# The last projection groups of an attention layer: spread over four tiles instead of three

## The chip, the cores and the metric

The kernel runs on one core of a Trainium2 chip. The time is that of one execution on the device, in microseconds (us). The core has five engines that run side by side, each taking its instructions in the order written for it: TensorE (PE, matrix products; PEld is its weight load), VectorE (DVE), ScalarE (ACT), GpSimd (POOL), and SyncE (SP), which here issues all transfers between the chip's outer memory and the memory beside the engines. Products land in a small accumulator memory of eight banks, which PE writes and DVE and ACT read.

## The reference

The model is a two-layer encoder over 1024 tokens of width 1024. Only layer 0 matters here, a differential attention with 8 heads:

```python
h = _rmsnorm(x, norm_g) * (1.0 + scale) + shift
q, k, v, z = jnp.split(h @ w_in, ...)          # 1024 columns each; q and k get a rotary embedding
sc = einsum('bqhcd,bkhcd->bhcqk', q, k) * scale # two score maps c = 0, 1 for each head
p = softmax(sc)
p = p[:, :, 0] - lam * p[:, :, 1]
o = einsum('bhqk,bkhd->bqhd', p, v)
o = _rmsnorm(o, subln_g) * (1.0 - lambda_init)
y = (o * silu(z)) @ w_out                       # then x = x + gate * y
```

All of it is float32. The kernel splits each float32 operand into a rounded high part and a rest, and forms a product from three: high x high, high x rest, rest x high.

## The kernel before

**Tiles.** The attention of layer 0 runs head by head. A head has 8 tiles of 128 queries (numbered 0 to 7); 4 tiles make a half of 512 queries. For each tile `q_tile` (from line 859) forms two score maps of 128 x 1024 on PE (L869, `s`). For each map DVE takes the negated maximum (L415, `nm`) and ACT the exponentials with their sum (L417). DVE then combines the two maps into one (L877, `e`). The combined tile is turned by PE, 128 x 128 at a time (L398, `tr`), ACT and DVE copy it out as a high part and a rest (L400 `pth`, L401 `ptl`), and when two tiles are turned, PE multiplies them with the values (`pv`, 24 products of three kinds, L173 to L175). This follow-up work of a tile, the class `Tail`, runs one and two tiles behind its scores, so the pv products fall into the odd tiles.

**Projection groups as filler.** The projections of later heads are cut into groups of three products of 512 columns (`gen_half`, written `acc` in the trace). A group is one step of the generator `stream0`. A table of six numbers for each tile says how many groups are written at six places of it: place 0 before the turning that follows the first score map, 1 after it, 2 after the second score map, 3 after the turning of the previous tile, 4 between the two parts of pv, 5 behind them. `FILL0` is the table for heads 0 to 6, `FILL7` that of the last head, where 13 groups are left: 5 for the first half of the tokens and 8 for the second. They form the gate projection z of head 7. When a half is complete, `silu_gate` makes the gate from it: a tanh on ACT (L804, `zth`) and a combination on DVE (L805, `gz`).

**What is done beside it in the last head.** `extra0(i)` is called at the end of tile i. At the end of tile `Z_LAST` it runs the rest of the stream and gives up the token memory: the pools that hold the normed tokens `h0` (64 KB in each partition) and the projection's scratch are closed, and pools for the output projection (`xp`, `pw`) are opened in their place. Then it starts the loads for the first of seven block products of the output projection (the class `Seven`: `fetch_a` loads activations, `fetch_w` weights, both L1183; `split_a` and `split_w` make the high part on ACT, L1202 `oah` and `woh`, and the rest on POOL, L1203 `oal` and `wol`). `PRE0` says how many steps of these products (`Pre7.step`, written `oy`) run at the end of each tile from tile 4 on; each is three products of 512 columns. SP's loads here are held in program order.

**Normalization of a head.** When a half of a head is finished, ACT squares it (L934, `osq`), PE sums the squares (L949, `ssq`), DVE and POOL make the factor, and SP sends it out and back as a broadcast (L423 `bc_d`, L425 `bc_s`). For the second half of head 6 this falls at the end of tile 2 of head 7.

**Order.** The order of each engine's instructions is written by a scheduler from its own cost estimates. It follows the order of the program only roughly. `behind("S")`, `behind("V")`, `issue_after` and `in_turn` tie single instructions to others: the casts of the output projection are put behind the latest softmax instruction on ACT, for example.

Of the kernel before, what the change touches and what calls it, by code (L numbers as in the profile page):

```python
# [48 lines left out]
PRE0 = (0, 0, 0, 0, 1, 2, 2, 3, 2, 2, 2)  # L49
PRE1 = (0, 0, 0, 0, 0, 0, 0, 1, 1, 1, 1)  # L50
LAST1 = (((0, 1), 0, HF), ((2,), 0, HF), ((3,), 0, 256), ((3,), 256, HF))
Z_LAST = 2
FILL7 = ((0, 1, 2, 1, 1, 0),) + ((0, 1, 1, 1, 1, 0),) * 2
G_WAIT = 5
G1_AT = 7
VB = (3, 3)
# [25 lines left out]
def trunk(ctx: ExitStack, tc: tile.TileContext, A, out):  # L82
# [946 lines left out]
    def attn0(h, fills, extra=None, late=None):  # L1029

        def close(half, o_, zz):
            if late and half == 1:
                ctx_["late"] = late(o_, zz)
                return
            o = a0b.tile([P, HF], F32, name="o", tag="o", bufs=2)
            sq = a0b.tile([P, HF], F32, name="osq", tag="osq", bufs=4)
            head_out(o_, o, sq, h, half)
            subln(o, sq, zz, half, h, None)

        ctx_ = dict(pool=a0b, l=0, h=h, open=lambda half: None, close=close)  # L1040
        for qp in range(4):
            half = qp // 2
            if qp % 2 == 0:
                zz = first.pop(0) if first else sm.tile([P, 4], F32, name="zz")
            for t in range(2):
                fl = fills(qp * 2 + t)

                def fill(i):
                    if fl[i]:
                        stream0.step(fl[i])  # L1050

                def mid(c):
                    if c == 0:
                        fill(0)
                        if tails[0]:
                            tails[0].turn(1)
                        fill(1)

                if first:
                    e0 = first.pop()  # L1060
                else:
                    e0 = q_tile(h, half, (qp * 2 + t) % 4, zz, a0b, mid)
                    fill(2)
                    after_scores(fill, 3)
                side.tick()
                tails[:] = [tails[1], Tail(qp, t, e0, zz, ctx_)]
                if extra:
                    extra(qp * 2 + t)
        if late:
            run_tails(lambda i: extra(8 + i))  # L1070
            while hooks:
                hooks.pop(0)()
            return ctx_["late"]
# [223 lines left out]
    def extra0(i):  # L1297
# [3 lines left out]
        if i == 1:  # L1301
            sv0.fetch_w(0, 0)
        if i < Z_LAST:
            return
# [13 lines left out]

        if i == Z_LAST:
            stream0.step(99)  # L1320
# [66 lines left out]

    tail0 = attn0(NH - 1, lambda i: FILL7[i] if i <= Z_LAST else (0,) * 6, extra0, late0)
    SP.dma_start(k0["12"], oF[0][NH - 1, 0])
# [1067 lines left out]
```

## Time and profile before

| what | value |
|---|---|
| median of 3 runs | 1389.32 us (1387.46 to 1389.65) |
| profiled execution, its own time | 1386.7 us |
| its span, first to last instruction | 1384.8 us |
| granted TensorE clock, mean | 0.996 |
| PE busy | 1362.2 us, 98% of the span |
| DVE, ACT, POOL busy | 940.0, 736.5, 701.6 us |

A row of the busy view by stretch gives the stretch, its length, and the busy time with the number of instructions of each engine, then the granted clock, the share of the transfer engines and GB/s. A timeline row gives start, length, engine, line, operation, tiles out<-in, shapes, count, and in brackets the idle time of the engine before it with what ended that. The chain of waits is the work that ended last, followed back; its rows have start, length and what. On PE the rows overlap, since products are pipelined: in the chain a product of 512 columns has 0.23 us, in the timeline 0.39. All starts are in us from the first instruction.

### The profile page before, as it was taken

Reading aid. Unit: us, or ns where it says so; the run is one execution under the profiler, and the core shown is the slowest. Engines: PE = TensorE matmul, PEld = TensorE weight load, DVE = VectorE, ACT = ScalarE, POOL = GpSimd, SP = SyncE. Lnnn points to the kernel's source line nnn. Section 1 sums busy time; section 2 is a strip of 40 time slices with the busy share of each in tenths; the row PEclk is TensorE's granted clock in tenths of the full one; section 3 lists DMA queues with packets and bytes.
Section 4 is the critical chain, followed back from the end, with each engine's and each line's share of the span. In section 5 each row is a group of like instructions: output and inputs, shape, how many; then the busy total and the mean of one; then the engine's idle time right before and its main releaser. Section 6 shows DMA issues by size and latency. Waiting matters only on the chain.

```text
span 1384.8 us, 20703 instructions
## 1 busy us (share of the span) xinstructions
PE 1362.2 (98%) x7334; PEld 1145.7 (83%) x7334; DVE 940.0 (68%) x1324; ACT 736.5 (53%) x1356; POOL 701.6 (51%) x550
## 2 busy tenths in 40 slices
PE   8999999999999999999999999999999999999997
PEld 6788888888888888887887888888888888888886
DVE  7654788877777767778596977545566555555684
ACT  5532465665565656566648543445454454545554
POOL 5434263646575757465694143531141373834674
PEclk9999999999999999999999999999999999999999
DMA  9857644344444434525654246499343463566463
GB/s 345 264 178 230 204 116 140 104 145 107 152 131 144 136 120 134 156 69 186 222 189 167 62 145 212 154 283 281 109 117 111 110 214 124 191 219 217 150 241 122
DMA packets 149387, 232.07 MB, mean 168 GB/s; under 512 B 20641, under 2 KB 57633, under 8 KB 149282
## 3 DMA queue, kind: packets, MB, share of 16 engines
q1 hardware_dynamic: 149282, 230.74, 52.4%
q8 instruction: 58, 0.95, 0.3%
q14 instruction: 47, 0.39, 0.1%
HBM read 144.74 MB, written 61.81 MB: 149 GB/s over the span
## 4 chain that ended last, share of the span: by engine, by line
PE 85%; DVE 6%; ACT 3%; DMA 3%; issue 2%; POOL 1%; SPq 1%; POOLq 0%; DVEq 0%; ACTq 0%
PE s L2071 10%; PE acc L173 9%; PE acc L175 9%; PE acc L174 9%; PE tr L398 8%; PE s L869 8%; PE pv L173 4%; PE pv L174 4%; PE pv L175 4%; DMA ada<-in_ada_ss 2%; PE oy L173 1%; PE oy L175 1%; PE oy L174 1%; PE zacc L174 1%; PE zacc L173 1%
## 5 line engine op out<-in xcount | busy, mean ns | idle before, releaser
L400 ACT CAST pth<-tr 128x512 fp32r<-128x512 f32 x256 | 150.3, 587 | 288.6 <-PE tr L398 283.8
L401 DVE TENSOR_TENSOR ptl<-tr,pth 128x512 fp32r<-128x512 f32 x256 | 176.2, 688 | 147.5 <-ACT pth L400 143.4
L415 DVE TENSOR_REDUCE nm<-s 128x1 f32<-128x1024 f32 x192 | 233.9, 1218 | 52.4 <-PE s L869 42.8
L219 POOL TENSOR_TENSOR wl<-wraw,wh 128x512 fp32r<-128x512 f32 (+2 forms) x77 | 102.6, 1333 | 278.7 <-ACT wh L218 201.0
L417 ACT ACTIVATE e<-s,nm 128x1024 f32<-128x1024 f32 x128 | 143.5, 1121 | 37.6 <-DVE nm L415 37.1
L398 PE MATMUL tr<-ident,e 128*128 128x128 f32 x1024 | 154.8, 273 | 3.0 <-DVE ptl L401 2.7
L398 PEld LDWEIGHTS tr<-ident,e 128*128 128x128 f32 x1024 | 121.1, 140 | 43.8 <-DVE ptl L401 21.0
L173 PE MATMUL acc<-h0h,wh 128*128 128x512 f32 x360 | 149.5, 415 | 0.0
L173 PE MATMUL pv<-pth,vt 128*128 128x256 f32 x512 | 147.6, 288 | 0.0
L174 PE MATMUL pv<-ptl,vt 128*128 128x256 f32 x512 | 145.7, 284 | 0.0
L175 PE MATMUL pv<-pth,vt 128*128 128x256 f32 x512 | 144.6, 282 | 0.0
L175 PE MATMUL acc<-h0h,wl 128*128 128x512 f32 x360 | 141.9, 394 | 0.0
L174 PE MATMUL acc<-h0l,wh 128*128 128x512 f32 x360 | 141.2, 392 | 0.0
L173 PEld LDWEIGHTS pv<-pth,vt 128*128 128x128 f32 x512 | 97.2, 190 | 2.7 <-ACT pth L400 0.2
L174 PEld LDWEIGHTS pv<-ptl,vt 128*128 128x128 f32 x512 | 97.4, 190 | 2.5
L1203 POOL TENSOR_TENSOR wol<-wol,woh 128x512 fp32r<-128x512 f32 x56 | 82.6, 1497 | 29.8 <-ACT woh L1202 28.1
L175 PEld LDWEIGHTS pv<-pth,vt 128*128 128x128 f32 x512 | 97.4, 190 | 0.1
L869 PE MATMUL s<-ks,qa 128*128 128x512 f32 x256 | 82.5, 401 | 2.4 <-DVE e L877 2.3
L877 DVE SCALAR_TENSOR_TENSOR e<-s,z,e 128x1024 f32<-128x1024 f32 x64 | 82.2, 1284 | 2.2
L175 PEld LDWEIGHTS acc<-h0h,wl 128*128 128x128 f32 x360 | 67.6, 188 | 14.9
L869 PE MATMUL s<-ks,qb 128*128 128x512 f32 x256 | 79.7, 392 | 0.0
L174 PEld LDWEIGHTS acc<-h0l,wh 128*128 128x128 f32 x360 | 68.2, 189 | 9.2
(429 smaller groups left out, 3390.2 us busy)
## 6 DMA issues: line engine op xcount, KB each, us to landing
ada<-in_ada_ss SPq DMA_DIRECT2D x32, 512.0 KB, 6.1
wraw<-in_w_s SPq DMA_DIRECT2D x64, 256.0 KB, 2.8
vS<-v_hl SPq DMA_DIRECT2D x32, 512.0 KB, 5.7
vt<-vS SPq DMA_DIRECT2D x32, 512.0 KB, 4.6
wol<-tS SPq DMA_DIRECT2D x56, 256.0 KB, 5.3
tS<-ob SPq DMA_DIRECT2D x48, 256.0 KB, 2.0
rp_sw<-rp_raw SPq DMA_DIRECT2D x160, 64.0 KB, 2.0
bc_s<-bc_d SPq DMA_DIRECT2D x34, 256.0 KB, 3.8
```

Of the source, the lines that this page charges most:

```text
L173: PE.matmul(psum, ah, bh, start=first, stop=False, skip_group_check=skip)
L174: PE.matmul(psum, ah, bl, start=False, stop=False, skip_group_check=skip)
L175: mm3.last = PE.matmul(psum, al, bh, start=False, stop=last, skip_group_check=skip).ins
L219: sub = (V if pair_of else G).tensor_sub(l_[:, :n], raw[:, :n], f32v(h_[:, :n]))
L398: transpose_p.last = PE.transpose(tr[:, j, :], p[:, kt * P : (kt + 1) * P], ident).ins
L400: mk["S"] = S.copy(pth[kh][:, :, dst], tr).ins
L401: mk["V"] = V.tensor_sub(ptl[kh][:, :, dst], tr, f32v(pth[kh][:, :, dst])).ins
L415: mk["V"] = V.reduce_max(nm, s_ps, axis=AX.X, negate=True).ins
L417: mk["S"] = S.activation(e, s_ps, AF.Exp, bias=nm, scale=1.0, accum_out=zs).ins
L869: PE.matmul(s_ps[:, kc * HF : (kc + 1) * HF], src[:, c, ql], KS[h][kc][:, c, :], start=fst, stop=not fst)
L1203: sub = eng.tensor_sub(lo, raw, f32v(hi))
L2071: PE.matmul(s_ps[:, kc * HF : (kc + 1) * HF], lhs, rhs(kc), start=i == 0, stop=i == 4)
```

## The change

Two constants. The first projection group moves out of the pair at place 2 of tile 0, one group at place 4 leaves tiles 1 and 2, and tile 3 gets three groups. The sums by tile go from 5, 4, 4, 0 to 4, 3, 3, 3. `Z_LAST` goes from 2 to 3: what `extra0` does at that point, closing the pools, two loads of activations, one of weights and the split of one weight tile, is done at the end of tile 3, ahead of the loads that stand there already.

```diff
-Z_LAST = 2
-FILL7 = ((0, 1, 2, 1, 1, 0),) + ((0, 1, 1, 1, 1, 0),) * 2
+Z_LAST = 3
+FILL7 = ((0, 1, 1, 1, 1, 0),) + ((0, 1, 1, 1, 0, 0),) * 3
```

The two places that read them:

```python
tail0 = attn0(NH - 1, lambda i: FILL7[i] if i <= Z_LAST else (0,) * 6, extra0, late0)
...
if i < Z_LAST:
    return
...
if i == Z_LAST:
    stream0.step(99)
    side.flush()
    stW.close()
    stH.close()
    ...
    fa(0, 0, 1)
    fw(0, 1)
    sv.split_w(0, 0)
if i == 3:
    fw(0, 2)
    fa(0, 2)
    fw(0, 3)
```

## The prediction

> **What bounds the kernel now.** I read the page first, for the span and the chain that ended last.
>
> ```profile
> span 1384.8 us, 20703 instructions
> ...
> PE 1362.2 (98%) x7334; PEld 1145.7 (83%) x7334; DVE 940.0 (68%) x1324; ACT 736.5 (53%) x1356; POOL 701.6 (51%) x550
> ...
> PE 85%; DVE 6%; ACT 3%; DMA 3%; issue 2%; POOL 1%; SPq 1%; POOLq 0%; DVEq 0%; ACTq 0%
> ```
>
> TensorE carries 85% of the chain. Whatever the change gives must come out of stretches where TensorE waits. So the next view is the busy time by stretch, cut where the first score product of each tile of the last head starts on PE (tiles 0 to 4 of eight):
>
> ```profile
> core 0: us, PE busy (x) PEld busy (x) DVE busy (x) ACT busy (x) POOL busy (x), PEclk, DMA share, GB/s
> 613.22:619.40 6.18, 6.18 (x34) 5.11 (x33) 3.48 (x5) 3.50 (x7) 4.08 (x3) 1.00 0.09 20
> 619.40:627.77 8.37, 8.37 (x53) 7.39 (x52) 7.54 (x10) 5.18 (x9) 7.74 (x6) 1.00 0.67 220
> 627.77:634.08 6.31, 6.31 (x39) 5.35 (x37) 4.58 (x6) 4.39 (x8) 0.00 (x0) 1.00 0.36 125
> 634.08:640.37 6.29, 5.87 (x43) 5.28 (x42) 5.51 (x10) 3.19 (x7) 1.85 (x3) 1.00 0.22 36
> 640.37:645.50 5.13, 3.36 (x19) 2.16 (x17) 4.64 (x7) 2.86 (x7) 2.19 (x2) 1.00 0.89 256
> ```
>
> In tiles 0 to 2, which hold the thirteen groups, PE is busy all the time; in tiles 3 and 4 it has gaps. The same view over longer stretches, before, during and after the part without projection groups:
>
> ```profile
> 590.00:634.08 44.08, 44.08 (x259) 38.08 (x258) 32.80 (x46) 28.34 (x51) 26.22 (x22) 1.00 0.31 90
> 634.08:666.48 32.40, 28.87 (x177) 23.75 (x177) 27.67 (x41) 23.66 (x47) 18.92 (x17) 1.00 0.58 179
> 666.48:711.00 44.52, 44.46 (x222) 37.17 (x221) 30.95 (x37) 24.73 (x50) 37.63 (x27) 1.00 0.72 260
> ```
>
> So PE is full, then has 32.40 - 28.87 = 3.53 us of gaps in tiles 3 to 7, then is full again. Time won before 666 us is handed on whole: behind it PE has 0.06 us of gaps in 44.52 us. The chain of waits through this place tells who sets the pace, and prices the pieces (start, length, what):
>
> ```profile
> 627.69 0.12 PE pv L174
> ...
> 629.99 0.93 PE s L869 x4
> ...
> 631.61 0.44 PE tr L398 x4
> 632.05 0.23 PE acc L173
> 632.28 0.23 PE acc L174
> 632.51 0.24 PE acc L175
> ...
> 633.43 0.80 PE ssq L949 x8
> ...
> 636.18 0.59 DVE gz L805
> ...
> 639.15 0.51 ACT woh L1202
> ```
>
> Up to 634.2 us the chain is PE; from there on it is the softmax on DVE and ACT. One projection group is three products, 0.23 + 0.23 + 0.24, taken as 0.69 us (the next rows have 0.23 for the third).
>
> **The change, part by part.** (1) Tiles 0, 1 and 2 lose one group each: 3 x 0.69 = 2.07 us of PE work, and as PE is full there, that is the most the softmax of tile 3 can come forward by this. How much does come forward is read on DVE, at the combination of the two exponentials (L877, one in each tile) and at the waits ahead of it:
>
> ```profile
> 626.76 1.28 DVE L877 SCALAR_TENSOR_TENSOR e<-s,z,e 128x1024 f32<-128x1024 f32 x1
> 628.60 0.75 DVE L938 SCALAR_TENSOR_TENSOR o<-pv,g,gz 128x512 f32<-128x512 f32 x1 [0.56 <-ACT osq L934]
> ...
> 634.25 0.16 DVE L954 SCALAR_TENSOR_TENSOR sl_w<-ssq,sl_w 128x4 f32<-128x4 f32 x1 [0.86 <-PE ssq L949]
> ...
> 634.90 1.28 DVE L877 SCALAR_TENSOR_TENSOR e<-s,z,e 128x1024 f32<-128x1024 f32 x1
> ...
> 641.79 1.28 DVE L877 SCALAR_TENSOR_TENSOR e<-s,z,e 128x1024 f32<-128x1024 f32 x1
> ```
>
> In tile 1 DVE is busy 7.54 of 8.37 us, so a shorter PE there helps little. In tile 2, DVE waits twice for work that stands behind the groups on PE: 0.56 us for the square of the finished head (ACT, released by the last pv product) and 0.86 us for the sums ssq. Both get shorter as PE comes forward. 0.56 + 0.86 = 1.42 us, less than 2.07. I take **-1.4 us** at tile 2's combination; the bounds are 0 and -2.07.
>
> (2) Tile 3 gains three groups, 2.07 us of PE work. Its own work is two scores, two transposes and 24 pv products: 2 x 0.93 + 2 x 0.44 + 24 x 0.12 = 5.6 us in a tile of 6.29 us: room for 0.69 us. The rest, 1.4 us, pushes the first score of tile 4, which now starts at 640.37; with PE 2.07 us early it would start at 640.37 - 0.69 = 639.7 and end 0.93 later at 640.6. DVE needs it when tile 3's combination ends, now 643.08, then 641.7. So 1.1 us of cover is left, and the term is **0**. What PE does today in that place is waiting (row at 643.13):
>
> ```profile
> 643.13 0.73 PE L869 MATMUL s<-ks,qa 128*128 128x512 f32 x2 [1.24 <-DVE e L877]
> ...
> 648.07 0.50 PE L175 MATMUL oy<-woh,oal 128*128 128x512 f32 x1 [0.51 <-POOL oal L1203]
> ```
>
> If that cover were gone, only tile 3's room would pay, and the gain would be 0.7 us. [...]
>
> (3) Two short pieces that stand on the chain in tile 3 move on with the steps. The gate of the second half (gz, 0.59 on DVE) follows the last group, now in tile 3; the first weight cast (woh, 0.51 on ACT), made where the token memory is given up, goes to the end of tile 3. Tile 3's softmax gets 1.10 us shorter and tile 4's as much longer, if nothing hides them there. Bounds -1.10 and 0; I take **0**, since tile 4's chain runs over the same two engines. Tile 4 also takes the subtraction of that cast on POOL, which is not on the chain today.
>
> (4) The loads into the freed memory (two of activations, one of weights) move behind tile 3, into the queue where the four of that tile already stand. SP's rows, then ACT's and POOL's, then the landing times of these activation loads:
>
> ```profile
> 637.89 0.32 SPq L425 DMA_DIRECT2D bc_s<-bc_d  x1
> 638.26 2.37 SPq L1183 DMA_DIRECT2D oal<-oF  x2
> ```
>
> ```profile
> 646.03 0.62 ACT L1202 CAST oah<-oal 128x512 fp32r<-128x512 f32 x1
> ```
>
> ```profile
> 639.74 1.30 POOL L1203 TENSOR_TENSOR wol<-wol,woh 128x512 fp32r<-128x512 f32 x1 [3.94 <-ACT woh L1202]
> ```
>
> ```profile
> DMA to landing us min/median/max: 3.1/4.8/5.2
> ```
>
> Although the memory is free at 633.4 (the last group), the loads go out at 638.26: SP takes its instructions in order and stands at the broadcast bc_s, which follows ssq. In the new order the last group ends at about 637.5 (tile 3's PE start 632.0, then two scores, two transposes, three groups and some pv products), and bc_s is 1.4 to 2 us earlier. So the loads go out at about the same time as now. Their first cast is wanted at 646.03 - 1.4 = 644.6; the first load lands at most 5.2 us behind its issue, at 643.5. With 1.1 us to spare the term is **0**; its upper bound is the third rival. What stands behind the casts on ACT is the second exponential of tile 4.
>
> The written order of PE is made anew by the scheduler. Its waits in tiles 3 to 7 today (0.4 to 0.6 us each, as in the row at 648.07) may come or go: +-0.6.
>
> **Sum**: -1.4 + 0 + 0 + 0 = -1.4 us, 1383.4 us of span. The profiled run took 1386.7 us, 1.9 more than its span; the median of the runs, 1389.32, lies 2.6 above that. I forecast 1389.32 - 1.4 = **1387.9**. A change of 0.2% (2.8 us) is about what can be told from none here, so this is no change that a measurement shows. The forecast's own range is -2.6 (2.07 and 0.6 of order) to -0.1 (0.7 less 0.6): 1386.7 to 1389.2.
>
> **Rivals.** *The pieces leave the chain for good.* The full 2.07 us comes forward and gz and woh find gaps in tile 4 (there DVE is busy 4.64 of 5.13 us, ACT 2.86): -2.07 - 1.10 = -3.2, **1386.1**. For it: ACT has 2.3 us of gaps there. Against it: tile 1, where DVE and not PE looks full.
>
> *The softmax already sets tiles 0 to 2.* Then nothing comes forward, and tile 3's PE work of 5.6 + 2.07 = 7.7 us outgrows its 6.29: +1.4, **1390.7**. For it: DVE's 7.54 of 8.37 in tile 1. Against it: the two DVE waits in tile 2 and the chain, which is PE there.
>
> *The memory comes free too late (the slower side).* If the loads wait for the last gate and not for the last product, they start when gz ends. By step 3 gz runs behind tile 3's combination, as it runs behind tile 2's today (634.90 to 636.18 + 0.59, 1.87 us from the combination's start): 641.79 - 1.4 + 1.87 = 642.3, or 4.0 us later than 638.26. The first load lands at up to 642.3 + 5.2 = 647.5 and the cast slips to 1.5 us behind its present 646.03, with the softmax behind it on ACT. POOL has one subtraction more, 1.30, ahead of the first output product, and PE's transposes stand behind that product, which waits for POOL by 0.51 us even now. 1.5 + 1.3 = +2.8, **1392.1**. It decides once the loads go out after 646.03 - 5.2 = 640.8. [...] Against it: the activation buffers freed first lie where the earliest tokens lay, and the gate's scratch is not among them. That the later release does nothing at all is likely for the same reason: SP, not the memory, holds the loads back today.
>
> **Chances.** Forecast 0.55, pieces leave 0.17, softmax sets 0.16, too late 0.12. Faster by over 0.2%: the first rival and little of the forecast's edge, 0.18. Slower: the last rival and little of the second, 0.13. Within: 0.69. For 8 in 10 the range takes in the first two rivals and 1.1 us beyond them, half the spread of the three runs (1387.46 to 1389.65): 1385.0 to 1391.8.
>
> **What would show it.** The combination of tile 2 at about 633.5 (now 634.90) shows step 1; PE's 1.24 us wait ahead of tile 4's second score gone or under 0.6 shows step 2; gz between the combinations of tiles 3 and 4 shows step 3; the loads out at 637 to 639, and no cast waiting for DMA, show step 4. PE's gaps of 3.53 us in tiles 3 to 7 should fall to about 2. I am wrong if tile 2's combination stays within 0.4 us of 634.90, if PE shows gaps in tiles 0 to 2 that eat the 2.07, or if ACT waits for a load in tile 4.

## The result, and the profile after

The changed kernel takes 1386.61 us (median of 20 executions, 1384.77 to 1388.99), the kernel before 1388.58 us beside it (20 executions, 1386.86 to 1390.87). The ratio is 0.9987, with a 95% interval of 0.9981 to 0.9993. By the ratio that is 1.8 us less, with an interval of 1.0 to 2.6 us (the medians differ by 1.97): a gain that 20 executions of each tell from none, but inside the 0.2% of the forecast.

Both spans hold a part that the two kernels share, and it does not always take as long. So the traces are compared by one stretch, **S**: from the start of tile 0's first score product in head 7 to the start of tile 7's combination. Its first and last rows, on PE and DVE, in the timeline of the kernel before:

```profile
613.22 0.63 PE L869 MATMUL s<-ks,qa 128*128 128x512 f32 x2
...
668.14 1.28 DVE L877 SCALAR_TENSOR_TENSOR e<-s,z,e 128x1024 f32<-128x1024 f32 x1
```

The same two in the changed kernel, and between them DVE's combinations of tiles 2 and 3 (L877), with DVE's one wait in tile 2 and the copy that is written behind it:

```profile
615.46 0.40 PE L869 MATMUL s<-ks,qa 128*128 128x512 f32 x1
...
634.64 0.16 DVE L954 SCALAR_TENSOR_TENSOR sl_w<-ssq,sl_w 128x4 f32<-128x4 f32 x1 [1.30 <-PE ssq L949]
634.72 0.68 DVE L401 TENSOR_TENSOR ptl<-tr,pth 128x512 fp32r<-128x512 f32 x1
635.32 0.15 DVE L955 SCALAR_TENSOR_TENSOR sl_f<-sl_f,ssq 128x4 f32<-128x4 f32 x1
635.38 0.16 DVE L875 RECIPROCAL z<-z 128x1 f32<-128x1 f32 x1
...
635.88 1.28 DVE L877 SCALAR_TENSOR_TENSOR e<-s,z,e 128x1024 f32<-128x1024 f32 x1
...
642.61 1.28 DVE L877 SCALAR_TENSOR_TENSOR e<-s,z,e 128x1024 f32<-128x1024 f32 x1
...
668.98 1.28 DVE L877 SCALAR_TENSOR_TENSOR e<-s,z,e 128x1024 f32<-128x1024 f32 x1
```

S is 668.14 - 613.22 = 54.92 us before and 668.98 - 615.46 = 53.52 after: **-1.40 us**. Starts of the combinations, counted from tile 0's first score:

| tile | 0 | 1 | 2 | 3 | 4 | 5 | 6 | 7 |
|---|---|---|---|---|---|---|---|---|
| before | 6.19 | 13.54 | 21.68 | 28.57 | 35.08 | 41.60 | 48.38 | 54.92 |
| after | 6.55 | 13.07 | 20.42 | 27.15 | 33.66 | 40.18 | 46.98 | 53.52 |
| difference | +0.36 | -0.47 | -1.26 | -1.42 | -1.42 | -1.42 | -1.40 | -1.40 |

All of it is made by tile 3's combination. Behind S, the two traces take 716.66 and 716.92 us to the end of the span. Ahead of S they differ by 615.46 - 613.22 = 2.24 us, which is not the change's: the code there is the same, and the kernel before alone begins head 7 anywhere from 612.45 to 615.10 us in its three profiles. This is why the two profiled spans (1384.8 and 1385.9) stand the wrong way round.

The busy view by stretch of the changed kernel, cut at the places that answer to those of the prediction (the ends of the middle stretch are tile 3's first score and the first output product after tile 7's scores):

```profile
590.00:634.46 44.46, 44.46 (x261) 38.21 (x260) 34.23 (x46) 28.70 (x51) 28.44 (x23) 1.00 0.33 96
634.46:667.31 32.85, 30.77 (x186) 25.45 (x186) 28.37 (x42) 24.81 (x49) 18.91 (x17) 1.00 0.55 176
667.31:711.84 44.53, 44.47 (x222) 37.20 (x221) 31.00 (x37) 24.78 (x50) 37.64 (x27) 1.00 0.74 260
```

PE's gaps in tiles 3 to 7 are 32.85 - 30.77 = 2.08 us, where they were 3.53. The stretches around it are as full as before, so the time won is handed on.

PE in tiles 3 to 5 of the changed kernel: the second score of tile 3 (behind all three of its groups, whose last product starts at 637.77), the second score of tile 4, and the first output product that waits for POOL:

```profile
638.00 0.61 PE L869 MATMUL s<-ks,qa 128*128 128x512 f32 x2
...
643.95 0.73 PE L869 MATMUL s<-ks,qa 128*128 128x512 f32 x2 [0.21 <-DVE e L877]
...
648.89 0.50 PE L175 MATMUL oy<-woh,oal 128*128 128x512 f32 x1 [0.52 <-POOL oal L1203]
```

Before, the chain of waits leaves PE at 634.2 us, ahead of tile 2's combination. In the changed kernel it stays on PE a tile longer, up to the turn in tile 3:

```profile
638.16 0.91 PE s L869 x4
...
639.90 0.45 PE tr L398 x4
...
640.38 0.59 ACT pth L400
```

The gate and its neighbours on DVE in tile 3:

```profile
639.11 1.23 DVE L415 TENSOR_REDUCE nm<-s 128x1 f32<-128x1024 f32 x1 [0.21 <-PE s L869]
640.25 0.68 DVE L805 SCALAR_TENSOR_TENSOR gz<-zth,acc 128x512 f32<-128x512 f32 x1
641.00 0.69 DVE L401 TENSOR_TENSOR ptl<-tr,pth 128x512 fp32r<-128x512 f32 x1
```

ACT's casts of the output projection, with what stands before and behind the first of them:

```profile
640.38 0.59 ACT L400 CAST pth<-tr 128x512 fp32r<-128x512 f32 x1
...
641.96 0.62 ACT L1202 CAST woh<-wol 128x512 fp32r<-128x512 f32 x1
643.77 0.59 ACT L400 CAST pth<-tr 128x512 fp32r<-128x512 f32 x1 [1.20 <-PE tr L398]
...
646.86 0.62 ACT L1202 CAST oah<-oal 128x512 fp32r<-128x512 f32 x1
```

And the loads, in SP's rows:

```profile
638.40 0.32 SPq L425 DMA_DIRECT2D bc_s<-bc_d  x1
638.77 0.90 SPq L1183 DMA_DIRECT2D oal<-oF  x2
```

### The profile page after: what moved, and what is told of

The parts are those of the page before. It is cut to its first block, busy times and chain, and to the rows that moved or that the text cites. A ratio compares the mean times of both kernels' runs of the same rounds, so it can differ in the third digit from the quotient of the medians.

```text
span 1385.9 us, 20703 instructions
## 1 busy us (share of the span) xinstructions
PE 1362.4 (98%) x7334; PEld 1145.2 (83%) x7334; DVE 938.9 (68%) x1324; ACT 737.7 (53%) x1356; POOL 699.6 (50%) x550
## 4 chain that ended last, share of the span: by engine, by line
PE 80%; DVE 6%; DMA 4%; ACT 3%; POOL 2%; issue 2%; SPq 1%; POOLq 0%; ACTq 0%; DVEq 0%
PE s L2071 10%; PE acc L175 9%; PE acc L173 8%; PE acc L174 8%; PE tr L398 8%; PE s L869 7%; PE pv L173 4%; PE pv L175 4%; PE pv L174 4%; PE oy L173 1%; PE oy L175 1%; PE oy L174 1%; DMA ada<-in_ada_ss 1%; PE zacc L175 1%; PE zacc L174 1%
## 5 line engine op out<-in xcount | busy, mean ns | idle before, releaser
L219 POOL TENSOR_TENSOR wl<-wraw,wh 128x512 fp32r<-128x512 f32 (+2 forms) x77 | 99.7, 1296 | 282.5 <-ACT wh L218 211.1
L877 DVE SCALAR_TENSOR_TENSOR e<-s,z,e 128x1024 f32<-128x1024 f32 x64 | 82.2, 1284 | 2.2
```

The costliest lines, as they stand in the source:

```text
L219: sub = (V if pair_of else G).tensor_sub(l_[:, :n], raw[:, :n], f32v(h_[:, :n]))
```

## The experiments

A single execution cannot show 1.4 us: head 7 began between 612.45 and 615.54 us in the profiles below, ahead of any edit. So what each kernel is judged by is S and its parts. All kernels compute the whole reference. The edits are shown against the changed kernel. All starts of combinations are counted from tile 0's first score product; the rows are in the order in which they are discussed.

| kernel | groups in tiles 0 to 3 | tile 0 | tile 1 | tile 2 | tile 3 | tile 6 | tile 7 (S) | one execution, us |
|---|---|---|---|---|---|---|---|---|
| before | 5, 4, 4, 0 | 6.19 | 13.54 | 21.68 | 28.57 | 48.38 | 54.92 | 1386.7 |
| before, second profile | 5, 4, 4, 0 | 6.19 | 13.54 | 21.68 | 28.57 | 48.65 | 55.19 | 1388.91 |
| before, third profile | 5, 4, 4, 0 | 6.19 | 13.52 | 21.66 | 28.55 | 48.36 | 55.80 | 1386.84 |
| changed | 4, 3, 3, 3 | 6.55 | 13.07 | 20.42 | 27.15 | 46.98 | 53.52 | 1387.74 |
| changed, second profile | 4, 3, 3, 3 | 6.55 | 13.07 | 20.42 | 27.13 | 46.95 | 54.50 | 1387.65 |
| release alone | 5, 4, 4, 0 | 6.19 | 13.54 | 21.68 | 28.81 | 49.08 | 55.61 | 1389.21 |
| one group from tile 2 | 5, 4, 3, 1 | 6.19 | 13.54 | 21.10 | 27.76 | 47.58 | 54.11 | 1385.83 |
| one group from tile 0 | 4, 4, 4, 1 | 6.55 | 13.07 | 21.21 | 27.73 | 47.55 | 54.09 | 1388.39 |
| one group from tile 1 | 5, 3, 4, 1 | 6.20 | 13.54 | 20.97 | 27.49 | 47.31 | 54.75 | 1389.51 |
| the same again | 5, 3, 4, 1 | 6.19 | 13.55 | 21.00 | 27.52 | 47.33 | 53.86 | 1387.12 |
| one each from 1 and 2 | 5, 3, 3, 2 | 6.19 | 13.54 | 20.41 | 27.26 | 47.08 | 53.61 | 1387.38 |
| late groups tied | 4, 3, 3, 3 | 6.55 | 13.07 | 20.39 | 27.25 | 49.75 | 56.28 | 1390.91 |
| first load twice | 4, 3, 3, 3 | 6.55 | 13.07 | 20.40 | 27.12 | 49.01 | 55.54 | 1390.10 |
| one more into tile 3 | 4, 3, 2, 4 | 6.55 | 13.07 | 21.06 | 27.33 | 49.82 | 56.35 | 1391.25 |

Single executions of the kernel before on the same chips lay at 1388.15 (beside the release and the three kernels with one group moved, without the repeat), 1388.80 (beside the tied, the doubled, the 5, 3, 3, 2 and the second profile of before) and 1387.93 (beside the rest).

### The release alone

The groups are put back to 5, 4, 4, 0; the release of the token memory, and the loads and the cast behind it, stay at the end of tile 3.

```diff
-FILL7 = ((0, 1, 1, 1, 1, 0),) + ((0, 1, 1, 1, 0, 0),) * 3
+FILL7 = ((0, 1, 2, 1, 1, 0),) + ((0, 1, 1, 1, 1, 0),) * 2 + ((0,) * 6,)
```

> Only the release moves: the groups stay 5, 4, 4 in tiles 0 to 2, tile 3 has none, and the pools are closed and the first loads started at the end of tile 3. Measured on the stretch S from tile 0's first score product to the start of tile 7's combination (54.92 us before, 53.52 after). My theory (the groups pay, the release does nothing, since SP held the loads back anyway): S 54.5 to 55.1. Rival (the weight cast and the gate leaving the chain pay): S 54.4 or less. Rival (late release costs, hidden in the total): S 55.4 or more.

Measured: tile 2's combination stays at 21.68, tile 3's comes 0.24 us later, tile 4's 0.46 us on top, and S is 55.61, or 0.69 us longer than before. So the release alone wins nothing. S lies above the 54.5 to 55.1 of the first theory, and in the range of the third, but not for its reason: no cast waits for a load, and two thirds of the 0.69 us are a fall of the clock, shown below. The 0.24 us stand on ACT in tile 3. The cast and the copy `pth` are both ahead of the second exponential, as before, but the copy now comes first, and it starts 0.24 us later than the cast did (26.07 and 25.83 us from tile 0's first score):

```profile
640.77 0.57 ACT L400 CAST pth<-tr 128x512 fp32r<-128x512 f32 x1
641.24 0.62 ACT L1202 CAST woh<-wol 128x512 fp32r<-128x512 f32 x1
641.76 1.09 ACT L417 ACTIVATE s<-s,nm 128x1024 f32<-128x1024 f32 x1
```

The 0.46 us are something else. The busy view by stretch of this kernel, in tiles 4 and 5, shows the granted TensorE clock (third column from the right) at half for some 3.4 us (0.50 in 646.58:648.34, 0.53 in 648.34:650.00, 1.00 behind it), and PE's rows there are longer (the turn of four blocks 1.11 us, not 0.66):

```profile
643.11:646.58 3.47, 1.47 (x8) 0.70 (x6) 3.40 (x6) 1.21 (x2) 1.59 (x2) 0.99 0.99 305
...
646.58:648.34 1.76, 1.76 (x6) 1.57 (x7) 1.07 (x1) 1.20 (x4) 0.00 (x0) 0.50 0.87 257
```

Ahead of the fall, PE was busy 1.47 of 3.47 us. This is taken up below, under the repeats.

### One group from one tile

Each of three kernels moves a single group to tile 3 (place 1), from tile 2, 0 or 1. The fourth moves one from tile 1 and one from tile 2. In order:

```diff
-FILL7 = ((0, 1, 1, 1, 1, 0),) + ((0, 1, 1, 1, 0, 0),) * 3
+FILL7 = ((0, 1, 2, 1, 1, 0), (0, 1, 1, 1, 1, 0), (0, 1, 1, 1, 0, 0), (0, 1, 0, 0, 0, 0))
```

> One group moves, from tile 2 to tile 3 (5, 4, 3, 1). My theory: the wait of 0.86 us for the sums in tile 2 shortens by up to one group, S 54.2 to 54.5 (0.4 to 0.7 less than 54.92). Rival (only full relief of all three tiles counts): S 54.9. Rival (tiles 0 and 1 are set by the softmax, all of the gain is made in tile 2): S 53.5 to 53.8.

```diff
+FILL7 = ((0, 1, 1, 1, 1, 0), (0, 1, 1, 1, 1, 0), (0, 1, 1, 1, 1, 0), (0, 1, 0, 0, 0, 0))
```

> One group moves, from tile 0 to tile 3 (4, 4, 4, 1). My theory: PE comes 0.69 us early into tile 2, both DVE waits there shorten, S 54.2 to 54.5. Rival (the softmax sets tiles 0 and 1, so that a group taken out there gives nothing): S 54.9.

```diff
+FILL7 = ((0, 1, 2, 1, 1, 0), (0, 1, 1, 1, 0, 0), (0, 1, 1, 1, 1, 0), (0, 1, 0, 0, 0, 0))
```

> One group moves, from tile 1 to tile 3 (5, 3, 4, 1). My theory: as for the group from tile 0, S 54.2 to 54.5. Rival (DVE, busy 7.54 of 8.37 us, sets tile 1): S 54.9.

```diff
+FILL7 = ((0, 1, 2, 1, 1, 0),) + ((0, 1, 1, 1, 0, 0),) * 2 + ((0, 1, 1, 0, 0, 0),)
```

> Groups 5, 3, 3, 2: one less than before in tiles 1 and 2, tile 0 left as it was. One group out of tile 1 alone brought tile 6's combination 1.07 us forward, one out of tile 2 alone 0.81, one out of tile 0 alone 0.83 with tile 0 itself 0.36 us later. If the relief adds up to the two DVE waits of 1.42 us: S 53.4 to 53.6. If it adds up freely: S 53.0 (54.92 - 1.07 - 0.81) to 53.2. Rival (two groups do not bring what three bring): S 53.8 or more.

Measured: one group less brings tile 2's combination forward by 0.58 us (from tile 2), 0.47 (tile 0) or 0.71 (tile 1). So the rival that a group from tile 0 or 1 gives nothing is out. S (54.11, 54.09, and 53.86 in the second profile of the kernel from tile 1) is a little below the 54.2 to 54.5 expected, since tile 3 gets shorter as well. One group each from tiles 1 and 2 brings 1.27 us at tile 2, nearly the sum of the two (0.71 + 0.58 = 1.29). With the third, from tile 0, the changed kernel has no more than that (1.26).

DVE's rows in tile 2 show the waits. Before there are three: 0.56 us for the square, 0.86 for the sums ssq, and between them one that the prediction did not show, 0.49 for ACT's copy:

```profile
632.70 0.69 DVE L401 TENSOR_TENSOR ptl<-tr,pth 128x512 fp32r<-128x512 f32 x1 [0.49 <-ACT pth L400]
```

ACT itself waits 0.36 us there for PE's turn, so this wait too has PE behind it. With one group from tile 2, the wait for the square remains at 0.56 and the wait for ssq falls from 0.86 to 0.17 us:

```profile
633.64 0.16 DVE L954 SCALAR_TENSOR_TENSOR sl_w<-ssq,sl_w 128x4 f32<-128x4 f32 x1 [0.17 <-PE ssq L949]
```

With one group from tile 1 (the repeat of that kernel is shown) it is the other way round: no wait ahead of o, and ssq as before:

```profile
634.78 0.16 DVE L954 SCALAR_TENSOR_TENSOR sl_w<-ssq,sl_w 128x4 f32<-128x4 f32 x1 [0.86 <-PE ssq L949]
```

With one group from each, the wait ahead of o is gone, and two are left:

```profile
629.93 0.74 DVE L938 SCALAR_TENSOR_TENSOR o<-pv,g,gz 128x512 f32<-128x512 f32 x1
...
633.98 0.69 DVE L401 TENSOR_TENSOR ptl<-tr,pth 128x512 fp32r<-128x512 f32 x1 [0.45 <-ACT pth L400]
634.85 0.16 DVE L954 SCALAR_TENSOR_TENSOR sl_w<-ssq,sl_w 128x4 f32<-128x4 f32 x1 [0.17 <-PE ssq L949]
```

So these two groups cut DVE's waits in tile 2 from 1.91 to 0.62 us, and the combination comes 1.27 earlier.

The third group is not lost because the waits are used up: in the changed kernel DVE waits 1.30 us for ssq, more than before. PE's sums start at 633.27 us in the timeline before; their row in the changed kernel:

```profile
633.65 0.95 PE L949 MATMUL ssq<-ones,osq 128*128 128x1 f32 x8
```

Counted from tile 0's first score, the sums start at 20.05 us before and 18.19 after: 1.86 us of the 2.07 arrive there. One group from tile 0, 1 or 2 brings 0.47, 0.71 or 0.68 us at this place, and these add up to 1.86; with 5, 3, 3, 2 it is 1.38. But in the changed kernel the copy ptl, 0.60 us, is written behind the first of the two instructions that read the sums. In the kernels with 5, 3, 3, 2 and before it is written ahead of them, where DVE would wait anyway. 1.86 - 0.60 = 1.26, the measured gain. ACT's copy was done at 633.98, so the place is the written order's choice. Had ptl stood ahead, the next instruction (z) could have followed the exponential's sum, which ACT has at 635.08, and not have started at 635.38: the gain at tile 2 would have been about 1.56 us, an estimate from these rows that no kernel here tries.

In tile 0 the group has an effect of its own: that tile's combination comes 0.36 us later, because the copy of the turned tile (ptl) is now written ahead of it on DVE, and tile 1's comes 0.47 us earlier.

What is taken away has to be done in tile 3. From tile 2's combination to tile 3's it takes 6.89 us before, 6.52 with one group in tile 3 taken from tile 0 or 1, 6.66 with one from tile 2, 6.85 with two, 6.73 with three. With no group at all it is longest: there gz and woh both stand in that tile's chain. With one group from tile 0 or 1 only gz does; in the three other kernels the chain runs over PE to the turn in tile 3, and gz and woh are off it.

In the first profile of the kernel with one group from tile 1, S is 54.75 although tile 6 is 1.07 us ahead of before. The loss is in tile 7, in front of a cast on ACT:

```profile
668.02 0.62 ACT L1202 CAST oah<-oal 128x512 fp32r<-128x512 f32 x1 [0.81 <-DMA oal<-oF]
```

The cast waits 0.81 us for its load, and the second exponential stands behind it (668.55). That load landed 6.3 us after its issue; the one in its place landed after 5.2 us in the kernel before and 4.9 in the changed one. The same kernel was run again, without an edit:

> The kernel with groups 5, 3, 4, 1 once more, nothing edited. In its first profile ACT waited 0.81 us in tile 7 for a load that landed 6.3 us after its issue, and S was 54.75. If that landing was chance: no such wait, S 53.8 to 53.9. If the loads' places make it: the same wait and S near 54.7.

Measured: S 53.86, the load landed after 5.3 us, and no wait:

```profile
666.02 0.62 ACT L1202 CAST oah<-oal 128x512 fp32r<-128x512 f32 x1
```

So the late landing belongs to the execution, not to the place of the groups; below it appears in two other kernels as well.

### Groups late in tile 3, and loads late

Three kernels try to price what the third rival was about: groups or loads that come late. The first ties the second and third group of tile 3 behind the last score product (the condition takes in tile 2 too, where they stand behind it already):

```diff
-                    PE.matmul(s_ps[...], src[:, c, ql], KS[h][kc][:, c, :], start=fst, stop=not fst)
+                    q_tile.last = PE.matmul(s_ps[...], src[:, c, ql], KS[h][kc][:, c, :], start=fst, stop=not fst).ins
...
-                    if fl[i]:
+                    with tc.issue_after(q_tile.last) if i > 1 and (h, qp, fl[i]) == (NH - 1, 1, 1) else nullcontext():
```

> The changed kernel, with the second and third group of tile 3 tied behind that tile's second score product on PE (in the changed kernel all three stand ahead of it, and it starts 0.84 us after the combination that frees its banks). My theory (in tile 3 PE's order is what is left on the path): the second score of tile 3 starts within 0.2 us of the end of tile 2's combination, and S falls from 53.52 to 52.7 to 53.2. Rival (tile 3 is set by DVE and ACT anyway): S 53.4 to 53.6. Rival (the three groups then stand ahead of the transposes and hold up tile 4): S 53.9 or more.

The second makes the first activation load twice, the second time behind the first, so that the loads after it go out about 4 us later:

```diff
-            fa(0, 0, 1)
+            fa(0, 0), tc.keep_in_program_order(SP.dma_start(sv.raws[0, 0, "A"][2], oF[0][0, 0])), fa(0, 1)
```

> The changed kernel, with the first of the loads into the freed memory made twice, the second waiting for the first, so that its cast and the loads behind it come about one landing (4.8 us) later. My theory (the loads have about 1 us to spare, and behind a late cast on ACT stands the softmax): ACT waits 1.5 to 3 us for a load in tile 4, S 55.0 to 56.5. Rival (the loads have ample cover, when they start does not matter): S 53.4 to 53.7.

The third moves one more group from tile 2 to tile 3, at place 4:

```diff
-FILL7 = ((0, 1, 1, 1, 1, 0),) + ((0, 1, 1, 1, 0, 0),) * 3
+FILL7 = ((0, 1, 1, 1, 1, 0), (0, 1, 1, 1, 0, 0), (0, 1, 1, 0, 0, 0), (0, 1, 1, 1, 1, 0))
```

> Groups 4, 3, 2, 4 by tile: one more moves from tile 2 to tile 3, place 4. Theory that the combination of tile 2 comes forward only by what DVE waited there (1.42 us), and that a last group written late in tile 3 makes the scheduler turn the order of tiles 4 to 6 over: tile 2's combination at 20.4 from tile 0's first score, as with three groups, and S 55.5 to 56.3, lost between tiles 5 and 6. Rival, that PE sets tile 2 and the loss in the kernel with tied groups came of the tie: tile 2's combination at 19.7 to 20.0 and S 53.0 to 53.5.

Measured: S 56.28, 55.54 and 56.35, all 2.0 to 2.8 us longer than in the changed kernel and longer than before. Tile 3 hardly pays for it (its combination at 27.25, 27.12 and 27.33, against 27.15). From tile 4's combination to tile 5's it takes 0.57 us more than in the changed kernel, and from tile 5's to tile 6's about 8.5 us (8.51, 8.50 and 8.50) instead of 6.80. In none of them does a cast of tiles 3 to 7 wait for a load. So none of the three prices lateness by itself: in all of them the written order of tiles 4 to 6 has turned over, and what late groups or loads cost with the order kept stays untested. The tie did not do what its theory needed either: the second score of tile 3 starts 0.65 us after tile 2's combination ends, behind pv products that moved ahead of it, and not within 0.2.

The first weight cast (woh) moves too. It starts at 26.50 us from tile 0's first score in the changed kernel, and at 31.40, 30.68 and 31.48 in these three. POOL's subtractions follow it, and PE waits some 1.3 us for them ahead of the first output product, 0.52 in the changed kernel. Rows of the kernel with 4, 3, 2, 4 in tile 5, on PE and DVE:

```profile
650.48 0.50 PE L175 MATMUL oy<-woh,oal 128*128 128x512 f32 x1 [1.28 <-POOL oal L1203]
...
654.51 0.63 PE L398 MATMUL tr<-ident,e 128*128 128x128 f32 x4 [0.96 <-DVE ptl L401]
```

```profile
652.54 1.23 DVE L415 TENSOR_REDUCE nm<-s 128x1 f32<-128x1024 f32 x1 [1.67 <-PE s L869]
653.68 0.68 DVE L401 TENSOR_TENSOR ptl<-tr,pth 128x512 fp32r<-128x512 f32 x1
```

The changed kernel at the same place:

```profile
651.46 0.68 DVE L401 TENSOR_TENSOR ptl<-tr,pth 128x512 fp32r<-128x512 f32 x1
652.05 1.22 DVE L415 TENSOR_REDUCE nm<-s 128x1 f32<-128x1024 f32 x1
```

There DVE copies the turned tile while it would otherwise wait for the second score. In the turned order the copy is written behind the second maximum: DVE waits 1.67 us for the score, the score stands on PE behind an output product that waits 1.28 us for POOL, and PE's next turn then waits 0.96 us for the copy. The larger part is lost in tile 6. Its first maximum starts 3.69 us after tile 5's combination, 2.00 in the changed kernel, and waits for its score, whose last product stands on PE (658.81) behind six output products and the sums of a finished half:

```profile
659.24 1.22 DVE L415 TENSOR_REDUCE nm<-s 128x1 f32<-128x1024 f32 x1 [0.57 <-PE s L869]
```

Why the scheduler turns its order over is open: its cost estimates are in no trace.

The kernel with 4, 3, 2, 4 also speaks on tile 2. With one group less than the changed kernel in tile 2, its combination comes later there (21.06, not 20.42). The written order had changed in that place too: a group's product is now ahead of the turn, and DVE waits for ACT's copy, which waits for the turn (ACT's and DVE's rows of that place):

```profile
633.05 0.59 ACT L400 CAST pth<-tr 128x512 fp32r<-128x512 f32 x1 [1.44 <-PE tr L398]
```

```profile
633.67 0.69 DVE L401 TENSOR_TENSOR ptl<-tr,pth 128x512 fp32r<-128x512 f32 x1 [1.23 <-ACT pth L400]
```

Its first theory was right on the turned order and close on S (55.5 to 56.3, measured 56.35). Neither reading foresaw what happens in tile 2, so how far tile 2 could come forward without the change of order is not shown by it.

### The two kernels once more

> The kernel before once more, to see how well S repeats and whether the granted clock of TensorE stays full in tile 4, where PE has its longest gaps (with only the release moved it fell to 0.5 for 3.4 us there). If S is set by the written order: 54.8 to 55.0. If the clock falls here too: S about 0.5 more, with a granted clock of 0.5 in tiles 4 and 5.

> The changed kernel once more, nothing edited. The stretch S, from tile 0's first score product to tile 7's combination (54.92 us before, 53.52 after). If the gain of 1.40 us is of the order of the work: 53.5 within 0.3, and the granted TensorE clock 1.00 through tiles 4 and 5, as in the first profile of this kernel. If the fall of the clock to half that the second profile of the kernel before and the kernel with only the release moved showed in tiles 4 to 5 comes to this kernel as well: 53.8 or more and a stretch of about 3.4 us at 0.50.

> The kernel before, a third profile, nothing edited. If an empty tile 3 lets the clock fall in most executions: a stretch of about 3.4 us at 0.50 in tiles 4 to 5 and S near 55.2. If the fall was a chance event of one profile: clock 1.00 and S near 54.9.

Measured: up to tile 6 the three profiles of the kernel before give 48.38, 48.65 and 48.36 us, the two of the changed kernel 46.98 and 46.95. The gain of 1.4 us repeats. In tile 7, the changed kernel's second profile and the third of the kernel before each lose about 1 us to a late load. The second profile of the changed kernel:

```profile
666.88 0.62 ACT L1202 CAST oah<-oal 128x512 fp32r<-128x512 f32 x1 [0.92 <-DMA oal<-oF]
```

The load landed 6.4 us after its issue there, and 6.3 in the third profile of before (wait 0.81). With the first profile of the kernel with one group from tile 1 that makes three of the fourteen profiles, from three kernels.

The 0.27 us by which the second profile of before is longer at tile 6 are the fall of the clock again:

```profile
643.40:646.80 3.40, 1.63 (x9) 0.87 (x8) 3.37 (x5) 1.27 (x2) 1.52 (x1) 1.00 0.96 298
646.80:650.20 3.40, 3.40 (x11) 2.72 (x12) 1.93 (x4) 3.03 (x7) 1.28 (x1) 0.53 0.96 336
```

The first and third profile of before keep 1.00 through the same tiles, at the same PE busy time (here the first):

```profile
641.60:645.00 3.40, 1.63 (x8) 0.87 (x7) 3.37 (x5) 1.34 (x2) 1.44 (x1) 1.00 0.99 286
```

And the changed kernel, in its emptiest 3.4 us of these tiles:

```profile
642.40:645.80 3.40, 2.66 (x13) 1.68 (x13) 3.36 (x5) 1.50 (x3) 2.78 (x2) 1.00 1.03 382
```

Kernels whose tile 3 has no group leave PE busy for 1.40 to 1.63 of some 3.4 us (a stretch as long as the fall), less than half, and the clock fell in two of their four profiles. In the ten others the emptiest 3.4 us of tiles 3 to 7 hold 1.78 us or more (2.66 in the changed kernel), and the clock fell in none. That the groups in tile 3 keep the clock up fits this, but four profiles are few, and it was not tried on its own.

## Why the prediction was right, point by point

The forecast was 1387.9 us, 1.4 us below the median shown, with a change that cannot be told from none. Measured were 1.8 us (1.0 to 2.6) and 1386.61 us. The change is under 0.2%, as forecast, but its interval leaves out zero. Of the distance between 1387.9 and 1386.61, 0.7 us lie in the base: the kernel before has 1388.58 over 20 executions, not 1389.32. The direction, the size and PE's part in it were right; that the steps add up to -1.4 so closely is partly luck, as steps 1 and 2 show.

**What bounds the kernel.** Held. PE is full on both sides of tiles 3 to 7, and a gain made before is still there at tile 7, in every kernel whose order stayed as it was, where neither the clock fell nor a load came late.

**Step 1, the groups that leave tiles 0 to 2: -1.4 us at tile 2's combination.** Measured -1.26. The combination was to come at about 633.5; it comes at 635.88, less 2.24 for the later start of the head, 633.64. That PE's lateness in tile 2 was what the groups cost is borne out: each group brings PE's sums forward, and by 1.86 of the 2.07 us in all. The cap of 1.42 us is not. The step added up two of DVE's three waits (it left out the 0.49 for ACT's copy), and the waits did not simply vanish: in the changed kernel those for the square and the copy are gone, the one for ssq has grown from 0.86 to 1.30, and 0.47 us are already won at tile 1's combination, where the step saw little to gain. What kept -1.86 down to -1.26 is the place of one copy, 0.60 us, in the written order, which the step could not know. So -1.4 came close partly by luck. Only with two groups (5, 3, 3, 2) does the reckoning by waits come out: 1.29 us of waits less, 1.27 won. But the PE work of two groups, 1.38 us, lies close to that too.

**Step 2, three groups in tile 3: 0.** Tile 3 becomes 0.16 us shorter (6.89 to 6.73). The cover was PE's wait of 1.24 us ahead of tile 4's second score; it is now 0.21, so the groups eat almost all of it. The push came out as reckoned: tile 4's first score starts at 642.21, or 639.97 on the clock of the trace before, for 639.7 foreseen. What the step did not see is that the chain of tile 3 itself now runs over PE, to the turn at 640.35. Tile 3 is no longer than before because the chain loses gz and woh there; by how much the groups alone would lengthen it, no kernel here shows. The order was not as assumed: all three groups stand ahead of tile 3's second score (637.77 and 638.00), and DVE waits 0.21 us for that score.

**Step 3, gz and woh: 0.** The sum was right and the place wrong. gz was to run between the combinations of tiles 3 and 4. It stays inside tile 3, 640.25 to 640.93, between the second maximum and the copy ptl, which cannot begin before ACT has finished pth at 640.97: it lies in a wait. woh runs at 641.96, after the second exponential, where ACT then waits 1.20 us for PE. The step's bounds priced both as if they had to lie in somebody's chain; with the release moved and no groups in tile 3, both do lie in tile 3's, as before.

**Step 4, the loads: 0.** They go out at 638.77, or 636.53 on the clock of the trace before: 1.73 us earlier than there, and 0.5 earlier than the 637 to 639 expected. They follow the broadcast bc_s directly, which comes 1.73 us earlier (1.4 to 2 foreseen); the last group ends at about 638.16, ahead of it, and not at 637.5 + 2.24 = 639.7 as assumed. So SP holds them, as the step says, but by little: in the kernel with 4, 3, 2, 4 SP stands some 1.4 us between the two loads of activations (2.25 us for both, 0.90 in the changed kernel), and the last group's product starts there, at 639.49. The bound on their landing was too low: they land 5.7 us after their issue, not at most 5.2, and the first cast, at 646.86, still has 2.4 us to spare. No cast in tile 4 waits for a load. The 0.52 us that PE waits for POOL ahead of the first output product is unchanged from 0.51.

**The sum.** -1.26 at tile 2 and -0.16 in tile 3 give -1.42; S, at -1.40, has it all. Step 1 fell 0.14 us short of its -1.4, and tile 3, put at 0, made that up: the two misses cancel by luck. The measured 1.8 us agrees within its interval. If the fall of the clock in the kernel before is as frequent as the profiles hint, it adds about 0.1 us (0.27 us in one of its three profiles) that the prediction did not count.

**The rivals.** *The pieces leave the chain for good* would have shown -2.07 at tile 2; it shows -1.26. gz and woh did find gaps, but the time they leave in tile 3 is taken up by the groups. *The softmax already sets tiles 0 to 2* falls with tile 2's combination. *The memory comes free too late* is refuted at its root, the loads that wait for the last gate. In the kernel with 4, 3, 2, 4 the gate does run behind tile 3's combination, and the loads are gone by then:

```profile
637.75 2.25 SPq L1183 DMA_DIRECT2D oal<-oF  x2
640.06 0.90 SPq L1183 DMA_DIRECT2D wol<-tS  x2
```

```profile
641.56 1.28 DVE L877 SCALAR_TENSOR_TENSOR e<-s,z,e 128x1024 f32<-128x1024 f32 x1
642.76 0.68 DVE L805 SCALAR_TENSOR_TENSOR gz<-zth,acc 128x512 f32<-128x512 f32 x1
```

No run shows the 1.5 us that its price takes for a late cast in tile 4; in tile 7, with one group from tile 1, a cast waited 0.81 us for its load ahead of the second exponential, and S was 0.89 us longer than in the repeat (54.75 and 53.86). The price, +2.8 us, was met by something else: the turned order of the scheduler, +2.0 to +2.8 in three kernels. One piece of the rival is in it, PE's wait for POOL ahead of the first output product, but behind a cast written late, not a load. The prediction had given order +-0.6 us, from the PE waits of the trace before. That was too little: one more group in tile 3, two tied later, or a later load cost the whole gain and more, and this, not the memory, was the slower side that lay nearest.

## What to carry to other kernels

When filler is taken from a full engine, follow the time won to the engine that consumes its results, and look at all of that engine's waits and at what is written around them. Here two groups cut three waits by 1.29 us and gave 1.27. Three groups brought the producer 1.86 us forward and gave only 1.26, because a copy of 0.60 us stood behind the wait and no longer ahead of it. Filler is worth moving into a stretch only while the wait that covers it there lasts (here 1.24 us, of which 0.21 are left), and where a scheduler writes the order, a neighbouring version can fall by more than the whole gain, so its order has to be read again for each. Where single executions differ by more than the gain, compare the traces over one stretch that begins behind the shared part.

## What the runs showed of the hardware

The granted TensorE clock fell to about half (0.50 and 0.53 in the rows above) for about 3.4 us in two of the fourteen profiles: in the kernel with the release alone after PE had been busy 1.47 of 3.47 us, in the second profile of before after 1.63 of 3.40, in pieces. The longest single wait of PE on semaphores was 1.47 us in the one case and 1.23 in the other. The same 1.63 of 3.40 did not bring it down in the two other profiles of before, which kept 1.00. So a stretch in which PE was less than half busy, with no wait above 1.47 us, stood ahead of both falls, and in two other executions no fall followed such a stretch. What decides between the executions, no run here shows.

The same activation load of tile 7 took 4.9 to 5.3 us to land in eleven of the profiles and 6.3 to 6.4 in three, in kernels with the same loads around it. In these three the cast that is written ahead of the exponential waited 0.81, 0.92 and 0.81 us for it. Neither this nor the fall of the clock was expected. The late landing falls on the kernel before as well as on the changed one; the fall of the clock was seen only in the kernel before and in the one with the release alone.
